# A hybrid decoder block on one core: one value mix ahead of a weight split, a projection tile by halves, compression blocks in other places

## The chip, the cores and the metric

The kernel runs on one core of a Trainium2 chip. A core has a matrix engine (TensorE, PE in the profile), a vector engine (DVE), an activation engine (ACT), a general engine (GpSimd, POOL), and SyncE (SP), which here issues the weight transfers. Each engine runs its own instructions in order, and waits on the others by semaphores. The metric is the device time of one execution in microseconds; the number before is the median of three runs.

## What is computed

One layer of a decoder, for 512 tokens of width 1024, in fp32. A normalised input goes through one wide projection. Its columns feed a sparse attention mixer (queries, three kinds of keys and values), an RWKV-7 recurrence and two gates. Both mixers are projected, merged by the gates, projected again and added; a gated MLP with a short convolution follows.

```python
h = rmsnorm(x, attn_norm_g[l])
proj = h @ w_in[l]
q, k_c, v_c, k_s, v_s, k_w, v_w, nsa_gate, rwkv_in, gate_a, gate_b = jnp.split(proj, IN_SPLITS, axis=-1)
o_a = nsa_mixer(q, k_c, v_c, ...)
o_b = rwkv7_mixer(rwkv_in, ...)
merged = jax.nn.sigmoid(gate_a) * (o_a @ w_proj_a[l]) + jax.nn.sigmoid(gate_b) * (o_b @ w_proj_b[l])
x = x + (merged @ w_out[l]).astype(x.dtype)
h2 = rmsnorm(x, ffn_norm_g[l])
x = x + conv_ffn(h2, ...)
```

Two details matter for the change. In the recurrence every projected column is mixed with that of the token before:

```python
shifted = jnp.pad(p_in, ((0, 0), (1, 0), (0, 0)))[:, :-1]
xl = p_in + (shifted - p_in) * mu
```

And the compression of the attention's keys and values cuts the tokens into overlapping blocks of 32 with a stride of 16 (31 blocks), adds a position embedding to each, and maps the flattened block by a small network:

```python
blocks = blocks + pe[None, None, :, None, :]
flat = blocks.transpose(0, 1, 3, 2, 4).reshape(b, n_cmp, g, CMP_BLOCK * dh)
return jax.nn.gelu(flat @ w1) @ w2
```

## The kernel before

**Weights in two parts.** A product in fp32 is made of three in a reduced format. Each weight tile arrives as `raw` (512 KB, a DMA from SP); ACT copies its high part into `whi` and DVE or POOL subtracts to get the low part `wlo` (`wsplit_`, the subtraction is line 299). The inputs have the parts `hh` and `hl`, and TensorE adds up hh by whi, hl by whi and hh by wlo. `weight_tiles` lists all tiles in the order of their use, with the engine that makes the low part; `wnext` hands out the next one, and in doing so issues the load and the split of the ones behind it. Compression weights (`cmp_w1_*`) are used as they arrive, without a split.

**Order.** Most instructions are written in program order and placed by a scheduler. While `urgent` is filled, the splits get priority. Some stretches (`tc.manual_schedule`) fix the order on the engines they name.

**The stages around the change.** The kernel works through the recurrence's four pairs of heads (`p` = 0 to 3): `front`, `norms`, `receptance`, `values_of`, `values_tok`, `vectors`, `gram`. `values_of(p)` projects the values on TensorE and mixes them with their neighbours (`shift_mix`: ACT scales, then DVE's `stt`, line 137, makes `vx`); `values_tok(p)` turns `vx` into token order by four transposes on TensorE (line 531). `gram(p)` forms products, of which DVE writes the masked result into `AB` (line 128). Between the last pair's `values_of` and `values_tok` TensorE makes the projection of the compressed keys, `kcp`. After the last pair `windows` copies it on ACT into `Dc`, a part of `QK`, and the query projection `dense_tok(512, hh, hl)` follows. This takes four weight tiles of two row blocks each; a tile is multiplied into four PSUM banks, one for each 128 tokens, all high parts first and then all low parts. The banks come from a ring of four (`ps_mm`), shared with what came before.

Meanwhile DVE inverts small triangular matrices in `inv`: four stream transposes (line 614) and a loop of 31 steps (lines 616 to 622), then stream transposes (L723 into `Y1`, which lies in `sg1[:, 1:3]`; L728 from `AB`). TensorE and ACT finish the inverse (`below`, `left`), with the projection of the last keys (`kv_proj(1, 280)`, three tiles) filled in between. `norm_keys(0)` and `rstd` make norms on DVE (rows with `rs_m`, `rs_y`), by which POOL multiplies keys and queries (lines 714 and 773).

**Compression.** `compress` writes blocks `Rk` on DVE (line 128, sg<-QK,prm): for keys and values, two groups and two halves (`jh`), eight writes of 8 by 31 columns, and fills the last column with zero (line 790). Then come four passes `s4` over the first weight, of 16 matmuls each, with other projections between them. The places `sg0` and `sg1`, four strips of 512 columns each, later receive the gates (`siga`). `sg0` shares its memory with `spare`, the split weights of one query tile and one key tile. The keys' blocks lie in `sg1[:, 0:2]` and the values' in `sg1[:, 2:4]`.

Of the kernel before, what the change touches and what calls it, by code (L numbers as in the profile page):

```python
# [23 lines left out]
NT = S // 128  # L24
# [58 lines left out]
def hybrid_block(ctx: ExitStack, tc: tile.TileContext, A: dict, out: bass.AP):  # L83
# [52 lines left out]
    def stt(o, a, s, b, op0=ALU.mult, op1=ALU.add):  # L136
        v.scalar_tensor_tensor(o, a, s, b, op0=op0, op1=op1)  # L137
# [120 lines left out]
            yield from rows(A["w_down"][0], 512 * hf, 512, NF)  # L258

    wtiles = weight_tiles()  # L260
    loads, ahead, late, slots = [], [], [], itertools.count()
    def wload():
        nxt = next(wtiles, None)
        if nxt is not None:
# [17 lines left out]
    def wsplit_():  # L282
        if loads:
            raw, kt, n, eng = loads.pop(0)
            if eng is None:
                ahead.append(raw)
                return
            if type(eng) is tuple:
                eng = eng[1]
                hi, lo = (spare[:, i].rearrange("p (k n) -> p k n", n=n) for i in range(2))  # L290
                act(hi, raw)
            else:
                hi = wp.tile([128, kt, n], F32R, name="whi", tag="whi", bufs=2)
                if late:
                    late.pop()(hi, raw)
                else:
                    act(hi, raw)
                lo = wp.tile([128, kt, n], F32R, name="wlo", tag="wlo", bufs=2)
            eng.tensor_tensor(lo, raw, hi.bitcast(F32), op=ALU.subtract)  # L299
            ahead.append((hi, lo))  # L300

    def wnext(kt, n):
# [100 lines left out]
    def dense_fm(xh, xl, kt=KT):  # L403
        return run(dense_fm_g(xh, xl, kt))
# [25 lines left out]
    def shift_mix(p, m, dst):  # L430
        mu = col("rwkv_mu", m)
        act(dst, p, AF.Copy, scale=omm[:, m:m + 1])
        stt(dst[:, 1:], p[:, :-1], mu, dst[:, 1:])

    def t2(name, bufs=1):
        return tp.tile([128, S], F32, name=name, tag=name, bufs=bufs)
# [84 lines left out]

    def values_of(p):
        vx = t2("vx")
        shift_mix(dense_fm(hh, hl), 8 + p, vx)
        L[p]["vx"] = vx

    def values_tok(p):
# [94 lines left out]
        stt(Tn[:, k + 1:, 0:n], tmv, 1.0, Tn[:, k + 1:, 0:n], ALU.mult, ALU.add)  # L622


    def dense_tok_g(n, xh, xl, kt=KT):
        banks = [mmb() for _ in range(NT)]
        step = 1024 // n
        tiles = [list(range(k0, min(k0 + step, kt))) for k0 in range(0, kt, step)]

        def passes(parts, ts_):  # L630
            for part in range(2):
                for ks, w in parts:
                    for i, k in enumerate(ks):
                        for t in ts_:
                            qs = slice(128 * t, 128 * t + 128)
                            if part == 0:
                                mm(banks[t][:, 0:n], xh[:, k, qs], w[0][:, i], k == 0, False)
                                mm(banks[t][:, 0:n], xl[:, k, qs], w[0][:, i], False, False)
                            else:
                                mm(banks[t][:, 0:n], xh[:, k, qs], w[1][:, i], False, k == kt - 1)  # L640
                    if len(ts_) > 1:
                        yield

        for ks in tiles[:-2]:
            yield from passes([(ks, wnext(len(ks), n))], range(NT))
        last = [(ks, wnext(len(ks), n)) for ks in tiles[-2:]]
        for t in range(NT):
            yield from passes(last, [t])
            if t < NT - 1:
                yield  # L650
        return banks

    def dense_tok(*a, **kw):
        return run(dense_tok_g(*a, **kw))
# [18 lines left out]

    windows(0, kcp)
    urgent.append(1)
    bq = dense_tok(512, hh, hl)
    for t in range(NT):
        act(qn[:, t], bq[t])
        for h in range(H):
# [104 lines left out]


    def compress():
        Rk = [sg1[:, 2 * a:2 * a + 2].rearrange("p m s -> p (m s)").rearrange("p (j g n) -> p j g n", j=16, g=2)
              for a in range(2)]
        for a, s_ in enumerate("kv"):
            v.memset(Rk[a][:, :, :, 31:32], 0.0)  # L790
            r0 = ROWS["cmp_pe_" + s_][0]
            for g in range(2):
                dv = Dc[:, a, g].rearrange("p (n j) -> p j n", j=8)
                for jh in range(2):
                    tt(Rk[a][:, 8 * jh:8 * jh + 8, g, 0:31], dv[:, :, jh:31 + jh],
                       prm[:, r0 + 8 * jh:r0 + 8 * jh + 8, None].to_broadcast([128, 8, 31]), ALU.add)
        cw2, hid, hidT, kcd = (QK[:, o:o + 256] for o in range(3072, 4096, 256))
        cw2 = cw2.rearrange("p (a m d) -> p a m d", a=2, m=2)
        hidT = hidT.rearrange("p (m a n) -> p m a n", m=2, a=2)
        kcd = kcd[0:32].rearrange("p (g a d) -> p g a d", g=2, a=2)  # L800
        kcs = cp.tile([32, 2], F32, name="kcs")
        yield
        hx = mmb()[:, 0:256]
        for s4 in range(4):
            w = [wnext(4, 256) for _ in range(2)]
            for j in range(4):
                for a in range(2):
                    mm(hx[64 * a:64 * a + 64], Rk[a][:, 4 * s4 + j].rearrange("p g n -> p (g n)"), w[a][:, j],
                       s4 + j == 0, s4 + j == 6)
            if s4 == 2:  # L810
                for a, s_ in enumerate("kv"):
                    nc.sync.dma_start(cw2[:, a], A["cmp_w2_" + s_][0].rearrange("(m p) d -> p m d", p=128))
            yield
        act(hid, hx, AF.Square)
        ts(hid, hid, 0.044715, 1.0)
        tt(hid, hid, hx, ALU.mult)
        act(hid, hid, AF.Tanh, scale=math.sqrt(2.0 / math.pi))
        stt(hid, hid, 1.0, hx, ALU.add, ALU.mult)
        yield
        pt = mmb()  # L820
        for m in range(2):
            te.transpose(pt[:, 128 * m:128 * m + 128], hid[:, 128 * m:128 * m + 128], ident)
        act(hidT.rearrange("p m a n -> p (m a n)"), pt[:, 0:256])
        yield
        kc_ps = mmb()
        for g in range(2):
            for m in range(2):
                mm(kc_ps[0:32, 64 * g:64 * g + 64], hidT[:, m, 0, 32 * g:32 * g + 32], cw2[:, 0, m], m == 0, m == 1)
        nc.gpsimd.memset(vcb, 0.0)
        for g in range(2):  # L830
            for e in range(2):
                bs = slice(64 * g + 32 * e, 64 * g + 32 * e + 32)
                for m in range(2):
                    mm(kc_ps[bs, 128:192], hidT[:, m, 1, 32 * g:32 * g + 32], cw2[:, 1, m], m == 0, m == 1)
        for g in range(2):
            for e in range(2):
                bs = slice(64 * g + 32 * e, 64 * g + 32 * e + 32)
                act(vcb[bs, 2 * g + e], kc_ps[bs, 128:192], AF.Copy, scale=0.5)
        for g in range(2):
            act(kcd[:, g, 0], kc_ps[0:32, 64 * g:64 * g + 64], AF.Copy, scale=0.5)  # L840
            act(kcd[:, g, 1], kcd[:, g, 0], AF.Square, accum_out=kcs[:, g:g + 1])
        rstd(kcs, DH)
        for g in range(2):
            ts(kcd[:, g, 1], kcd[:, g, 0], kcs[:, g:g + 1], None)
            ts(kcd[:, g, 0], kcd[:, g, 0], kcs[:, g:g + 1], None)
        yield
        pt = mmb()
        for g in range(2):
            te.transpose(pt[:, 32 * g:32 * g + 32], kcd[:, g].rearrange("p a d -> p (a d)"), ident[0:32, 0:32])
        ptv = pt[:, 0:64].rearrange("p (g n) -> p g n", g=2)  # L850
        act(KC[:, :, 0], ptv, AF.Copy, scale=kg)
        stt(KC[:, :, 1], ptv, kg, KC[:, :, 0].bitcast(F32), ALU.mult, ALU.subtract)
# [366 lines left out]
    units += [(qt, g, (0, 1)) for qt in (1, 0) for g in range(2)]  # L1219
    nfill = [5, 5, 6, 6, 7, 8, 10, 10, 10, 9, 9, 6]  # L1220
    with tc.manual_schedule(engines=KTS):
        behind = (1,2,3,4,5,6,7,8,9)
        scores(units[0], 12)
        scale(units[0])
        comp = compressed(3)
        next(comp)
        scores(units[1], 12)
        for i, u in enumerate(units):
            turns(u)
            if i == 0:  # L1230
                run(comp)
            if i in (4, 8, 10):
                compressed_t(u[0])
            if i + 2 < len(units):
                mid = [lambda: None, functools.partial(scale, units[i + 1])] if i + 1 in behind else [lambda: None, lambda: None]
                if i == 0:
                    mid.insert(0, functools.partial(compressed_t, 3))
                scores(units[i + 2], nfill[i], mid)
                if i + 2 not in behind:
                    scale(units[i + 2])  # L1240
            else:
                filler(nfill[i])
            if i in (1, 5, 7):
                run(compressed({1: 2, 5: 1, 7: 0}[i]))
            values(u)
        filler(100)
# [155 lines left out]
```

## Time and profile before

| | |
|---|---|
| runs | 834.2, 834.1, 833.83 us |
| median | 834.1 us |
| profiled execution | 833.78 us, of which 831.9 us are the span of the trace |
| granted TensorE clock | 1.0 over the whole span |
| TensorE (PE) busy | 823.2 us |
| DVE, ACT, POOL busy | 514.4, 406.4, 51.5 us |

The span goes from the first to the last instruction of the trace; what lies around it, 1.9 us, is start and end. A row of a timeline has the start, the duration, the engine and line, the operation, output and inputs by their names, the tile and the type, and how many of the kind it holds; in brackets stand the idle time before it and what ended that. Matmuls overlap, so the distance between two starts tells more than the duration.

### The profile page before, as it was taken

Reading aid. Unit: us, or ns where it says so; the run is one execution under the profiler, and the core shown is the slowest. Engines: PE = TensorE matmul, PEld = TensorE weight load, DVE = VectorE, ACT = ScalarE, POOL = GpSimd, SP = SyncE. Lnnn points to the kernel's source line nnn. Section 1 sums busy time; section 2 is a strip of 40 time slices with the busy share of each in tenths; the row PEclk is TensorE's granted clock in tenths of the full one; section 3 lists DMA queues with packets and bytes.
Section 4 is the critical chain, followed back from the end, with each engine's and each line's share of the span. In section 5 each row is a group of like instructions: output and inputs, shape, how many; then the busy total and the mean of one; then the engine's idle time right before and its main releaser. Section 6 shows DMA issues by size and latency. Waiting matters only on the chain.

```text
span 831.9 us, 12894 instructions
## 1 busy us (share of the span) xinstructions
PE 823.2 (99%) x5107; PEld 669.9 (81%) x5107; DVE 514.4 (62%) x1006; ACT 406.4 (49%) x793; POOL 51.5 (6%) x67
## 2 busy tenths in 40 slices
PE   8999999999999999999999999999999999999998
PEld 7777778987777887787788988888888888888886
DVE  6577779974565878787665576556665556323222
ACT  6766655554455777685334554444444444221220
POOL 6100020140000200011000000000000000000000
PEclk9999999999999999999999999999999999999999
DMA  8432222246372310001275033333323332223421
GB/s 247 110 84 58 76 76 77 69 128 185 102 128 77 86 42 14 26 27 34 81 258 148 1 114 89 101 103 101 97 86 96 101 102 102 88 90 114 139 76 51
DMA packets 109400, 78.73 MB, mean 95 GB/s; under 512 B 3877, under 2 KB 98012, under 8 KB 109340
## 3 DMA queue, kind: packets, MB, share of 16 engines
q1 hardware_dynamic: 106800, 73.92, 30.2%
q10 hardware_dynamic: 1196, 2.55, 0.9%
q0 software_dynamic: 1344, 1.45, 0.8%
q8 instruction: 40, 0.66, 0.3%
q14 instruction: 20, 0.16, 0.1%
HBM read 74.56 MB, written 2.29 MB: 92 GB/s over the span
## 4 chain that ended last, share of the span: by engine, by line
PE 91%; DVE 5%; ACT 2%; issue 1%; DMA 0%; DVEq 0%; ACTq 0%
PE ps_mm L122 81%; PE ps_a L122 5%; PE ps_b L122 2%; PE ps_b L1196 1%; PE ps_mm L1196 1%; DVE AB L128 0%; DMA xt<-in_x_dram 0%; DVE P L1163 0%; DVE sC L128 0%; DVE wlo L299 0%; ACT P L125 0%; ACT L125 0%; ACT UV L125 0%; DVE P L132 0%; DVE PTs L1108 0%
## 5 line engine op out<-in xcount | busy, mean ns | idle before, releaser
L299 DVE TENSOR_TENSOR wlo<-raw,whi 128x1024 fp32r<-128x1024 f32 (+1 forms) x111 | 131.5, 1185 | 184.3 <-PE ps_mm L122 160.0
L122 PE MATMUL ps_mm<-hh,whi 128*128 128x512 f32 (+1 forms) x624 | 242.4, 391 | 0.5 <-DVE hl L137 0.5
L122 PE MATMUL ps_mm<-hl,whi 128*128 128x512 f32 (+1 forms) x624 | 240.2, 387 | 0.0
L125 ACT ACTIVATE whi<-raw 128x1024 fp32r<-128x1024 f32 (+3 forms) x124 | 123.3, 996 | 158.1 <-PE ps_mm L122 142.6
L122 PE MATMUL ps_mm<-hh,wlo 128*128 128x512 f32 (+1 forms) x624 | 152.1, 384 | 0.0
L122 PEld LDWEIGHTS ps_mm<-hh,whi 128*128 128x128 f32 x624 | 117.3, 188 | 27.2 <-issue 1.0
L122 PEld LDWEIGHTS ps_mm<-hl,whi 128*128 128x128 f32 x624 | 117.4, 188 | 23.0 <-issue 1.0
L122 PEld LDWEIGHTS ps_mm<-hh,wlo 128*128 128x128 f32 x624 | 115.1, 188 | 23.5
L122 PE MATMUL ps_mm<-whi,aT 128*128 128x512 f32 x352 | 84.5, 390 | 0.0
L122 PEld LDWEIGHTS ps_mm<-whi,aT 128*128 128x128 f32 x352 | 65.9, 188 | 14.3 <-issue 0.4
L137 DVE SCALAR_TENSOR_TENSOR cgv<-ps_mm,cw,cgv 128x511 f32<-128x511 f32 (+1 forms) x88 | 65.4, 746 | 1.6
L125 ACT ACTIVATE cgv<-ps_mm,cw 128x512 f32<-128x512 f32 x44 | 34.2, 780 | 23.3 <-PE ps_mm L122 23.3
L122 PE MATMUL ps_mm<-wlo,aT 128*128 128x512 f32 x176 | 44.3, 389 | 0.0
L125 ACT ACTIVATE aT<-cgv 128x512 fp32r<-128x512 f32 x22 | 13.9, 632 | 56.8 <-DVE cgv L128 56.8
L125 ACT ACTIVATE P<-P,nm 128x512 f32<-128x512 f32 (+3 forms) x64 | 35.4, 554 | 12.2 <-DVE nm L1163 12.0
L122 PEld LDWEIGHTS ps_mm<-wlo,aT 128*128 128x128 f32 x176 | 33.0, 188 | 6.9
L125 ACT ACTIVATE cgv<-cgv 128x512 f32<-128x512 f32 x22 | 13.9, 632 | 41.3 <-DVE cgv L137 41.2
L299 POOL TENSOR_TENSOR wlo<-raw,whi 128x512 fp32r<-128x512 f32 (+3 forms) x13 | 20.7, 1593 | 200.9 <-PE ps_mm L122 132.2
L1163 DVE CUSTOM_DVE_ANT_0 P<-ps_a,AB 128x512 f32<-128x512 f32 (+3 forms) x64 | 29.3, 485 | 4.1 <-PE ps_a L122 4.0
L128 DVE TENSOR_TENSOR x<-x,ps_mm 128x512 f32<-128x512 f32 (+1 forms) x17 | 11.0, 655 | 22.8 <-PE ps_mm L122 20.6
L128 DVE TENSOR_TENSOR aT<-cgv,aT 128x512 fp32r<-128x512 f32 x22 | 15.3, 693 | 14.7 <-ACT aT L125 14.7
L125 ACT ACTIVATE QK<-ps_mm 128x64 f32<-128x64 f32 (+5 forms) x56 | 14.9, 309 | 18.4 <-PE ps_mm L122 18.3
(357 smaller groups left out, 1209.9 us busy)
## 6 DMA issues: line engine op xcount, KB each, us to landing
raw<-in_w_up_dram SPq DMA_DIRECT2D x44, 512.0 KB, 3.7
raw<-in_w_in_dram SPq DMA_DIRECT2D x38, 512.0 KB, 3.8
raw<-in_w_down_dram SPq DMA_DIRECT2D x22, 512.0 KB, 3.5
raw<-in_w_out_dram SPq DMA_DIRECT2D x8, 512.0 KB, 3.6
xt<-in_x_dram SPq DMA_DIRECT2D x4, 512.0 KB, 4.0
raw<-in_cmp_w_v_dram SPq DMA_DIRECT2D x4, 512.0 KB, 3.8
raw<-in_w_proj_b_dram SPq DMA_DIRECT2D x8, 256.0 KB, 2.6
raw<-in_w_proj_a_dram SPq DMA_DIRECT2D x8, 256.0 KB, 2.6
```

Of the source, the lines that this page charges most:

```text
L122: te.matmul(o, lhsT=l, rhs=r, start=start, stop=stop)
L125: sc.activation(o, i, f, **kw)
L128: v.tensor_tensor(o, a, b, op=op)
L137: v.scalar_tensor_tensor(o, a, s, b, op0=op0, op1=op1)
L299: eng.tensor_tensor(lo, raw, hi.bitcast(F32), op=ALU.subtract)
L1163: v.tensor_tensor_reduce(out=P[:, i], in0=sp[:, N * (i - i0):N * (i - i0) + N], in1=BT[:, h, 384 - 128 * qt:512], scale=-1.0, scalar=-NEG, ...
L1196: te.transpose(pt[:, 128 * i:128 * i + 128], P[:, 4 * x + i, 128 * k:128 * k + 128], ident)
```

## The change

Three things are changed. First, `shift_mix` returns its last instruction, and the weight split that comes after the values of the last pair gets an order edge behind it: on DVE `vx` stands ahead of the subtraction for the first query tile. Second, the first tile of the query projection is multiplied by two token tiles and then by the other two, high and low parts each time, instead of by all four. Third, the compression blocks have other places: the keys' halves in `sg0[:, 1]` and `sg0[:, 3]`, the values' in `sg0[:, 2]` and `sg1[:, 0]`, and each half has its own fill. By the built programs, two of the eight block writes stay in the inverse loop, and six, with three fills of 128 by 16, stand right behind the four transposes of L728 and ahead of the norms. The orders on ACT, POOL and SP are the same as before. A tuple in the attention loop has a new name.

```diff
-    loads, ahead, late, slots = [], [], [], itertools.count()
+    loads, ahead, late, behind, slots = [], [], [], [], itertools.count()
...
-            eng.tensor_tensor(lo, raw, hi.bitcast(F32), op=ALU.subtract)
+            low = eng.tensor_tensor(lo, raw, hi.bitcast(F32), op=ALU.subtract)
+            if behind:
+                tc.add_manual_dep(low.ins, behind.pop().ins.name, mybir.DependencyInfo(
+                    mybir.DependencyClass.NoSync, mybir.DependencyReason.DATA), reason="values of the last pair first")
...
-        stt(dst[:, 1:], p[:, :-1], mu, dst[:, 1:])
+        return v.scalar_tensor_tensor(dst[:, 1:], p[:, :-1], mu, dst[:, 1:], op0=ALU.mult, op1=ALU.add)
...
-        shift_mix(dense_fm(hh, hl), 8 + p, vx)
+        mixed = shift_mix(dense_fm(hh, hl), 8 + p, vx)
+        if p == NH2 - 1:
+            behind.append(mixed)
...
-    def dense_tok_g(n, xh, xl, kt=KT):
+    def dense_tok_g(n, xh, xl, kt=KT, halves=False):
...
-        for ks in tiles[:-2]:
-            yield from passes([(ks, wnext(len(ks), n))], range(NT))
+        for j, ks in enumerate(tiles[:-2]):
+            parts = [(ks, wnext(len(ks), n))]
+            for ts_ in ([range(2), range(2, NT)] if halves and j == 0 else [range(NT)]):
+                yield from passes(parts, ts_)
...
-    bq = dense_tok(512, hh, hl)
+    bq = dense_tok(512, hh, hl, halves=True)
...
-        Rk = [sg1[:, 2 * a:2 * a + 2].rearrange("p m s -> p (m s)").rearrange("p (j g n) -> p j g n", j=16, g=2)
-              for a in range(2)]
+        Rk = [[w.rearrange("p (j g n) -> p j g n", j=8, g=2) for w in ws]
+              for ws in ((sg0[:, 1], sg0[:, 3]), (sg0[:, 2], sg1[:, 0]))]
         for a, s_ in enumerate("kv"):
-            v.memset(Rk[a][:, :, :, 31:32], 0.0)
+            for w in Rk[a]:
+                v.memset(w[:, :, :, 31:32], 0.0)
...
-                    tt(Rk[a][:, 8 * jh:8 * jh + 8, g, 0:31], dv[:, :, jh:31 + jh],
+                    tt(Rk[a][jh][:, :, g, 0:31], dv[:, :, jh:31 + jh],
...
-                    mm(hx[64 * a:64 * a + 64], Rk[a][:, 4 * s4 + j].rearrange("p g n -> p (g n)"), w[a][:, j],
+                    mm(hx[64 * a:64 * a + 64], Rk[a][s4 // 2][:, 4 * (s4 % 2) + j].rearrange("p g n -> p (g n)"), w[a][:, j],
```

More of the change, by code (lines that the diff above doesn't have):

```diff
@@ L1221, in hybrid_block @@
     with tc.manual_schedule(engines=KTS):
-        behind = (1,2,3,4,5,6,7,8,9)
+        after_next = (1,2,3,4,5,6,7,8,9)
         scores(units[0], 12)
@@ L1234, in hybrid_block @@
             if i + 2 < len(units):
-                mid = [lambda: None, functools.partial(scale, units[i + 1])] if i + 1 in behind else [lambda: None, lambda: None]
+                mid = [lambda: None, functools.partial(scale, units[i + 1])] if i + 1 in after_next else [lambda: None, lambda: None]
                 if i == 0:
@@ L1238, in hybrid_block @@
                 scores(units[i + 2], nfill[i], mid)
-                if i + 2 not in behind:
+                if i + 2 not in after_next:
                     scale(units[i + 2])
```

## The prediction

> **What bounds the kernel.** I read the page's first part, then TensorE's timeline around each place that the change touches, then DVE, ACT and POOL at the same moments. TensorE is the bound:
>
> ```profile
> span 831.9 us, 12894 instructions
> ## 1 busy us (share of the span) xinstructions
> PE 823.2 (99%) x5107; PEld 669.9 (81%) x5107; DVE 514.4 (62%) x1006; ACT 406.4 (49%) x793; POOL 51.5 (6%) x67
> ```
>
> TensorE is busy for 823.2 of 831.9 us, so faster work elsewhere brings nothing by itself. Only the moments in which TensorE waits count. "Idle before" understates them, since pipelined matmuls overlap, so I take the distance from one start to the next and compare it with the same step where nothing is late. The first such place is the transposes of the last pair's values, against eight matmuls of the same kind 14 us earlier, behind which other transposes stand that were not late:
>
> ```profile
> 101.44 1.99 PE L122 MATMUL ps_mm<-hh,wlo 128*128 128x512 f32 x8
> 103.36 0.27 PE L562 MATMUL ps_b<-kc,bh 64*128 64x64 f32 x1
> ...
> 115.04 1.97 PE L122 MATMUL ps_mm<-hh,wlo 128*128 128x512 f32 x8
> 117.28 0.44 PE L531 MATMUL ps_b<-kc,vx 128*128 128x128 f32 x2 [0.26 <-DVE vx L137]
> ```
>
> The undisturbed step takes 103.36 - 101.44 = 1.92 us, this one 117.28 - 115.04 = 2.24. The wait is 0.32 us (the bracket shows 0.26 of it), released by DVE's vx. The second place is the first pass over the compression weights:
>
> ```profile
> 176.20 0.80 PE L122 MATMUL ps_mm<-wlo,hh 128*128 128x280 f32 x5
> ...
> 179.67 0.65 PE L122 MATMUL ps_mm<-raw,sg 128*64 128x256 f32 x2
> 180.51 1.94 PE L122 MATMUL ps_mm<-raw,sg 128*64 128x256 f32 x14 [0.19 <-DVE sg L128]
> 182.38 0.39 PE L122 MATMUL ps_mm<-whi,hh 128*128 128x280 f32 x1
> ...
> 197.22 1.95 PE L122 MATMUL ps_mm<-raw,sg 128*64 128x256 f32 x16
> 199.10 0.50 PE L122 MATMUL ps_mm<-hh,whi 128*128 128x512 f32 x1
> ```
>
> A later pass of the same 16 matmuls goes from 197.22 to 199.10, 1.88 us; this one from 179.67 to 182.38, 2.71. The wait is 0.83 us, of which the bracket shows only 0.19. Its releaser is the block that DVE writes into sg.
>
> **Part one: vx ahead of the split.** What DVE does before the transposes:
>
> ```profile
> 115.34 1.22 DVE L299 TENSOR_TENSOR wlo<-raw,whi 128x1024 fp32r<-128x1024 f32 x1
> 116.48 0.74 DVE L137 SCALAR_TENSOR_TENSOR vx<-ps_mm,prm,vx 128x511 f32<-128x511 f32 x1
> 118.83 0.69 DVE L128 TENSOR_TENSOR BO<-ps_a,vx 128x512 f32<-128x512 f32 x1 [1.61 <-PE ps_a L122]
> ```
>
> The split (wlo, 1.22 us) stands ahead of vx (0.74). In the other order vx ends near 116.1 instead of 117.22, ahead of the transposes' undisturbed start at 115.04 + 1.92 = 116.96. The whole 0.32 goes; the least I allow is the bracket's 0.26. The split moves back by 0.74 - less than BO's 1.61 us of idle time - and ends near 117.3. Its reader is the query projection, which starts after 121: hidden by four microseconds of recurrence products. No instruction is added; behind the new order edge on DVE stands only the split.
>
> **Part two: the query projection's first tile by two token tiles.** The same 24 matmuls go in another order; the third and fourth banks are touched first at places 13 and 15 instead of 7 and 11. The rows there, first TensorE's, then the DVE evacuation that frees banks two and three, then ACT's that frees the fourth:
>
> ```profile
> 119.21 0.22 PE L562 MATMUL ps_a<-kc,bh 64*128 64x64 f32 x1
> 119.57 0.37 PE L122 MATMUL ps_b<-AR,bh 64*128 64x128 f32 x1
> ...
> 122.12 0.40 PE L122 MATMUL ps_mm<-whi,hh 128*128 128x512 f32 x1
> 122.70 0.50 PE L122 MATMUL ps_mm<-whi,hh 128*128 128x512 f32 x1 [0.18 <-DVE AB L128]
> ...
> 123.52 0.39 PE L122 MATMUL ps_mm<-whi,hh 128*128 128x512 f32 x1
> ...
> 124.44 0.40 PE L122 MATMUL ps_mm<-whi,hh 128*128 128x512 f32 x1
> ```
>
> ```profile
> 121.97 1.28 DVE L128 TENSOR_TENSOR AB<-ps_mm,kc 128x512 f32<-128x512 f32 x2
> ```
>
> ```profile
> 121.75 1.06 ACT L125 ACTIVATE spare<-raw 128x1024 fp32r<-128x1024 f32 x1 [1.12 <-issue]
> 122.71 1.54 ACT L125 ACTIVATE QK<-ps_mm 64x256 f32<-64x256 f32 x4
> ```
>
> The wait that exists is at the second bank: 122.70 - 122.12 = 0.58, against a pace of 1.92 / 8 = 0.24, so 0.34 us. The new order keeps that matmul in fourth place, so the wait stays. Bank three is free at 121.97 + 1.28 = 123.25 and wanted at 123.52; bank four is free at 122.71 + 1.54 = 124.25 and wanted at 124.44. Neither is late, so this part is worth **0**. It becomes a cover: TensorE now comes 0.32 earlier, and if ACT's copy at 121.75 does not come earlier with it (what released it is not shown), bank four would be late by 0.32 - 0.19 = 0.13 us in the old order, and not in the new one. Value 0, bounds 0 to 0.13 of loss avoided, so the sum is not touched either way. The low half of the weight is now wanted at the ninth matmul instead of the seventeenth, after 123, and is done at 117.3.
>
> **Part three: the compression blocks' places.** Eight block writes of one kind stand on DVE:
>
> ```profile
> L128 DVE TENSOR_TENSOR sg<-QK,prm 128x248 f32<-128x248 f32 x8 | 5.0, 642 | 0.0
> ```
>
> ```profile
> 166.29 8.06 DVE L728 STREAM_TRANSPOSE AB<-inv 32x1024 f32<-32x1024 f32 x4
> 174.38 1.37 DVE L134 TENSOR_SCALAR rs_m<-kss 128x8 f32<-128x8 f32 x1
> 175.67 0.17 DVE L134 TENSOR_SCALAR rs_m<-qss 128x32 f32<-128x32 f32 x1
> ```
>
> Before, four of them run in the inverse loop and four follow the chain of norms, because their place is that of the inverse's transposes, which TensorE and ACT still use. After, two run in the loop and six stand right behind the four transposes (end 174.35), ahead of the norms, with three small fills that I bound by a small norm operation, 0.17 each. Six times 0.642 and three times 0.17 make 4.4 us. They start at the earliest at 174.35 - 0.32 - 2 x 0.642 (the two that leave the loop) = 172.8, at the latest at 174.35, so they end at 177.2 to 178.7. TensorE wants them at 179.67 - 0.32 = 179.35. Even the late end is 0.6 us ahead, and the **0.83 goes whole**.
>
> What is late next: the norms begin 2.8 to 4.3 us later than now and no longer beside the split, whose company cost them 1.2 (1.37 - 0.17); their end, which releases POOL, moves from 178.0 to 181 at most. POOL's rows:
>
> ```profile
> 174.33 1.39 POOL L299 TENSOR_TENSOR wlo<-raw,whi 128x560 fp32r<-128x560 f32 x1 [4.99 <-ACT AB L125]
> 178.02 2.65 POOL L714 TENSOR_TENSOR QK<-QK,kss 128x128 f32<-128x128 f32 x4 [2.30 <-DVE kss L137]
> 180.63 4.04 POOL L773 TENSOR_TENSOR QK<-QK,qss 128x512 f32<-128x512 f32 x4
> 192.65 1.48 POOL L714 TENSOR_TENSOR QK<-QK,kss 128x128 f32<-128x128 f32 x4 [7.97 <-DVE kss L137]
> ```
>
> POOL's eight multiplies (2.65 + 4.04) then end before 188, and its next work starts at 192.65: hidden, worth 0.
>
> The price that is new is POOL's split at 174.33. TensorE uses its result from the fourth matmul of the five at 176.20, at 176.20 + 3 x 0.13 = 176.6 (0.13 is half of 512-wide pace by 280 columns: 0.24 x 280 / 512), and 0.32 earlier after the first gain, 176.3. Today it runs beside small norms; after, beside block writes. Two rows show what that does: the same four POOL multiplies take 2.65 us beside block writes (178.02) and 1.48 alone (192.65), a factor of 1.8, while DVE's own 1.37 for a small operation beside the split, 0.17 otherwise, shows DVE giving way. If DVE gives way, the split costs TensorE nothing: released 0.32 earlier, it ends near 175.4, and with one block write ahead of it at 176.0. If POOL is slowed by 1.8, it ends at 174.0 + 2.5 = 176.5, 0.2 late. I take 0.1, between ends that are close.
>
> The Trainium skill ("SBUF — State Buffer", section "SBUF: two separate sides") says that DVE and GpSimd share one port pair under an exclusive lock, which whoever starts first holds for its whole instruction, DVE taking part also with two SBUF inputs against a GpSimd operation that reads SBUF. The 1.37 against 0.17 agrees; the slowed multiplies, beside which DVE's block writes were not slowed, agree only in part. By the rule POOL waits for one write, and the sum would be 0.1 larger than mine.
>
> **The sum.** -0.32 - 0.83 + 0.1 = -1.05 us. The profiled run took 833.78 (span 831.9), which becomes 832.7. The median of the runs is 834.1, 0.3 above the profiled one, and becomes **833.0**.
>
> **Rivals.** *More gain:* the other waits near these places go too, because DVE's and ACT's rows there come earlier by more than TensorE's. The step from 119.21 to 119.57 (0.36; two products of 64 columns are 0.06 at the same pace: 0.30 us) and the 0.34 at 122.70 would add 0.64, and with the 0.1 not paid: -1.8, 832.3. For it: a changed order on an engine often lets more than one wait go. Against: what releases them is work that follows the same TensorE transposes and so moves with them.
>
> *Given back at a transfer.* A later weight copy of ACT waits for its transfer:
>
> ```profile
> 197.55 1.06 ACT L125 ACTIVATE whi<-raw 128x1024 fp32r<-128x1024 f32 x1 [6.97 <-DMA raw<-in_w_in_dram]
> ```
>
> It ends at 198.61; TensorE wants it at 199.10. If the landing does not come earlier with TensorE, the 0.49 of slack holds and 1.05 - 0.49 = 0.56 is given back: -0.5, 833.6. Against: the buffer of that transfer is released by TensorE, so it is issued earlier too.
>
> *Slower:* POOL's split is starved by the six block writes until the last has ended. It then ends at 177.2 + 1.39 = 178.6 to 180.1, TensorE stalls for 2.3 to 3.8 us in the keys' projection (less the 0.1 of the sum), and the change costs +1.1 to +2.6: 835.2 to 836.7. It turns slower from the point where the split ends after 176.3 + 1.15 = 177.4. For it: the 2.65 against 1.48. Against: the multiplies at 178.02 did run beside the writes, at more than half pace.
>
> **Chances.** Forecast 0.56; more gain 0.24; given back 0.10; slower 0.10. The range goes from 832.1 to 834.3. A fifth of a per cent of 834.1, 1.7 us, is about what a measurement of this kernel can tell from no change: faster means under 832.4, slower over 835.8. The more-gain case lies around the first bound and mostly below it, the starved case around the second: faster 0.28, same 0.65, slower 0.07.
>
> **What would show it.** Right: vx ends before the eight matmuls do, and the step to the transposes takes 1.92; the first compression pass takes 1.88; the matmul at bank two keeps its 0.34. Wrong: POOL's split lengthened beyond 2.3 us or started late, with TensorE's gap inside the five at 176.20; a block write after TensorE's first compression matmul; a new gap ahead of 199.10 with ACT's copy as its releaser.

## The result and the profile after

| | before | after |
|---|---|---|
| median of 22 runs each | 833.83 us (833.49 to 834.2) | 832.61 us (832.28 to 832.93) |
| ratio, 95% interval | | 0.9985 (0.9979 to 0.999) |
| span of the profiled execution | 831.9 us | 830.7 us |

The change saves 1.22 us, 0.15%, inside the predicted range; the predicted saving was 1.05. Every run of the changed kernel lies below every run of the kernel before. The median is 0.4 us below the predicted 833.0, but 0.27 of that is the starting point: the prediction went from 834.1, the median of three runs, and the 22 runs have 833.83. The page of the changed kernel, span and busy time:

```profile
span 830.7 us, 12893 instructions
## 1 busy us (share of the span) xinstructions
PE 821.3 (99%) x5107; PEld 669.1 (81%) x5107; DVE 514.4 (62%) x1008; ACT 406.2 (49%) x793; POOL 50.7 (6%) x67
```

DVE's busy time is the same to the tenth of a microsecond, with two instructions more, and TensorE's count is the same: no work was taken away. (TensorE's busy time rests on modelled ends and cannot be read to a microsecond.) TensorE's timeline (start, duration, line, operation) shows that two waits are gone:

```profile
115.09 1.98 PE L122 MATMUL ps_mm<-hh,wlo 128*128 128x512 f32 x8
116.90 0.60 PE L536 MATMUL ps_b<-kc,vx 128*128 128x128 f32 x4
...
121.69 0.40 PE L122 MATMUL ps_mm<-whi,hh 128*128 128x512 f32 x1
122.27 0.50 PE L122 MATMUL ps_mm<-whi,hh 128*128 128x512 f32 x1 [0.19 <-DVE AB L128]
122.60 0.63 PE L122 MATMUL ps_mm<-whi,hl 128*128 128x512 f32 x2
...
175.74 0.80 PE L122 MATMUL ps_mm<-wlo,hh 128*128 128x280 f32 x5
...
179.22 1.95 PE L122 MATMUL ps_mm<-raw,sg 128*64 128x256 f32 x16
181.09 0.40 PE L122 MATMUL ps_mm<-whi,hh 128*128 128x280 f32 x1
...
197.87 0.50 PE L122 MATMUL ps_mm<-hh,whi 128*128 128x512 f32 x1
```

I read the gain by subtracting the starts of the same instructions in the two traces. At the eight low-part matmuls the changed kernel is 0.05 us later (115.09 against 115.04; the start of the first projection varies more than that, from 13.37 to 13.71 over all traces of this document). At 122.12, now 121.69, it is 0.43 earlier; at 176.20, now 175.74, 0.46; at 182.38, now 181.09, 1.29; at 199.10, now 197.87, 1.23. So the vx part brought 0.46 + 0.05 = about 0.5 us by then, the compression part 1.29 - 0.46 = 0.83, and 0.06 was lost again by 199.

DVE and POOL in the same stretch:

```profile
115.38 0.75 DVE L436 SCALAR_TENSOR_TENSOR vx<-ps_mm,prm,vx 128x511 f32<-128x511 f32 x1
116.04 1.22 DVE L299 TENSOR_TENSOR wlo<-raw,whi 128x1024 fp32r<-128x1024 f32 x1
...
173.32 3.81 DVE L128 TENSOR_TENSOR sg<-QK,prm 128x248 f32<-128x248 f32 x5
176.57 0.07 DVE L798 MEMSET sg<- 128x16 f32 x1
177.05 0.63 DVE L128 TENSOR_TENSOR sg<-QK,prm 128x248 f32<-128x248 f32 x1
```

```profile
173.88 1.78 POOL L299 TENSOR_TENSOR wlo<-raw,whi 128x560 fp32r<-128x560 f32 x1 [5.00 <-ACT AB L125]
180.03 1.47 POOL L721 TENSOR_TENSOR QK<-QK,kss 128x128 f32<-128x128 f32 x4 [4.36 <-DVE kss L137]
181.46 4.05 POOL L780 TENSOR_TENSOR QK<-QK,qss 128x512 f32<-128x512 f32 x4
191.71 1.47 POOL L721 TENSOR_TENSOR QK<-QK,kss 128x128 f32<-128x128 f32 x4 [6.20 <-DVE kss L137]
```

vx ends at 115.38 + 0.75 = 116.13, 0.77 us ahead of its transposes. The last block write ends at 177.05 + 0.63 = 177.68, 1.54 ahead of the first compression matmul at 179.22. POOL's split, 1.39 us long before, now takes 1.78 and ends at 175.66; TensorE wants it at 175.74 + 3 x 0.13 = 176.13.

### The profile page after: what moved, and what is told of

It reads as the page before. It is cut to its first block, busy times and chain, and to the rows that moved or that the text cites. A ratio compares the mean times of both kernels' runs of the same rounds, so it can differ in the third digit from the quotient of the medians.

```text
span 830.7 us, 12893 instructions
## 1 busy us (share of the span) xinstructions
PE 821.3 (99%) x5107; PEld 669.1 (81%) x5107; DVE 514.4 (62%) x1008; ACT 406.2 (49%) x793; POOL 50.7 (6%) x67
## 4 chain that ended last, share of the span: by engine, by line
PE 95%; DVE 3%; ACT 1%; DMA 0%; issue 0%; DVEq 0%; ACTq 0%
PE ps_mm L122 84%; PE ps_a L122 5%; PE ps_b L122 2%; PE ps_b L1204 1%; PE ps_mm L1204 1%; DMA xt<-in_x_dram 0%; DVE P L1171 0%; DVE sC L128 0%; ACT P L125 0%; DVE P L132 0%; PE ps_b L536 0%; PE ps_b L567 0%; DVE PTs L1116 0%; PE ps_a L1016 0%; PE ps_b L203 0%
```

## The experiments

All were compared with the kernel before in the same job; differences are those of the medians. "Full change" is the changed kernel, at 832.61 us. It was measured in a job of its own, and the median of the kernel before moved from 833.83 to 833.97 us between the jobs, so a difference to the full change is good to about 0.1 us.

**One part at a time.** Each of the first three kernels keeps one part of the change; the fourth leaves only the halves out. The diffs here and below are against the changed kernel.

```diff
 e1, e3, e4:
-    bq = dense_tok(512, hh, hl, halves=True)
+    bq = dense_tok(512, hh, hl)
 e2, e3:
-        if p == NH2 - 1:
-            behind.append(mixed)
 e1, e2:
-        Rk = [[w.rearrange("p (j g n) -> p j g n", j=8, g=2) for w in ws]
-              for ws in ((sg0[:, 1], sg0[:, 3]), (sg0[:, 2], sg1[:, 0]))]
+        Rk = [sg1[:, 2 * a:2 * a + 2].rearrange("p m s -> p (m s)").rearrange("p (j g n) -> p j g n", j=16, g=2)
+              for a in range(2)]
...
```

> Only the order edge that puts the last pair's vx ahead of the weight split. My theory: the three parts add up, and this one is worth the whole distance that TensorE gained at the transposes of vx: in the changed kernel the step from the eight low-part matmuls to them takes 116.90 - 115.09 = 1.81 us, before 117.28 - 115.04 = 2.24, so 0.43 us less time and the compression pass keeps its 2.71 us. By the prediction's own reference step (1.92) it would be 0.32. Rival: the 0.11 above that comes with another part (the halves), and this kernel shows a step of 1.92. Second rival: what TensorE gains here is lost again at bank four of the query projection, which is 0.13 us late without the halves, so 0.30.

> Only the query projection's first tile by two token tiles. My theory: no bank beyond the second was late, so the time is that of before within 0.1 us, and the wait at the second bank keeps its 0.34 us. Rival: the new order takes away a wait in the 24 matmuls that the rows did not show, and the time falls by 0.1 to 0.4 us.

> Only the new places of the compression blocks. My theory: the first compression pass takes 1.88 us instead of 2.71, and the time falls by 0.83 us; POOL's split beside the block writes takes about 1.8 instead of 1.39 us and is in time. Rival: POOL's split, which here is wanted 0.4 us later than in the full change, or a later transfer gives part back, and the time falls by 0.3 to 0.6.

> The full change without the halves. My theory: same as the full change, 1.2 us less than before, since in the changed kernel ACT's copy for bank four moved with TensorE. Rival, the halves as a cover: bank four is late by about 0.13 us, seen as a gap in the first 24 matmuls, and the time falls by 1.1 only.

| kernel | median, us | before in the same job | difference |
|---|---|---|---|
| e1, vx ahead of the split | 833.4 | 833.92 | -0.52 |
| e2, halves | 833.9 | 833.92 | -0.02 |
| e3, places of the blocks | 833.13 | 833.92 | -0.79 |
| e4, full change without the halves | 832.62 | 833.92 | -1.30 |

The parts add up: 0.52 + 0.79 = 1.31 is what the two give together. The intervals of the ratios (0.9985 to 1.0003 for e1, 0.9982 to 0.9999 for e3) are about as wide as the effects. Still, every run of e1 (at most 833.54) and of e3 (at most 833.36) lies below every run of the kernel before in that job (at least 833.56). Where the time went, the traces show. TensorE's timeline of e1:

```profile
115.18 1.98 PE L122 MATMUL ps_mm<-hh,wlo 128*128 128x512 f32 x8
117.00 0.60 PE L536 MATMUL ps_b<-kc,vx 128*128 128x128 f32 x4
...
179.34 0.65 PE L122 MATMUL ps_mm<-raw,sg 128*64 128x256 f32 x2
180.14 1.94 PE L122 MATMUL ps_mm<-raw,sg 128*64 128x256 f32 x14 [0.15 <-DVE sg L128]
182.01 0.40 PE L122 MATMUL ps_mm<-whi,hh 128*128 128x280 f32 x1
```

The step to the transposes is 117.00 - 115.18 = 1.82 without the halves, so the 0.11 above the predicted 0.32 belongs to the vx part, and the first rival falls; with 0.52 us gained, the second falls too. The compression pass still waits: 182.01 - 179.34 = 2.67. Of e3:

```profile
117.47 0.66 PE L534 MATMUL ps_b<-kc,vx 128*128 128x128 f32 x4 [0.27 <-DVE vx L436]
...
179.87 1.95 PE L122 MATMUL ps_mm<-raw,sg 128*64 128x256 f32 x16
181.75 0.40 PE L122 MATMUL ps_mm<-whi,hh 128*128 128x280 f32 x1
```

Here the wait on vx is back (0.27) and the pass takes 181.75 - 179.87 = 1.88; with 0.79 us gained, nothing much was given back. The halves alone change nothing, and with the rest, their absence (e4) costs nothing either. The cover that I allowed them was not needed, because ACT's copy in the changed kernel had moved with TensorE:

```profile
121.31 1.06 ACT L125 ACTIVATE spare<-raw 128x1024 fp32r<-128x1024 f32 x1 [1.12 <-issue]
```

121.75 became 121.31, 0.44 earlier like TensorE's own rows, so bank four kept its slack. In e4, which has no cover, that copy starts at 121.21, and from the fifth matmul of the tile on the steps are the usual 0.23: the third and fourth banks are not late.

**The two waits that were left.** The rival of more gain said that these go too. They did not by themselves: in the changed kernel the second bank still waits (122.27 - 121.69 = 0.58). The next three kernels take them away. e5 exchanges the banks in the last pair's gram:

```diff
-            ptr = [mmb(), mmb()] if c0 else [pb(), pa()]
+            ptr = [mmb(), mmb()] if (c0 > 0) != (p == NH2 - 1) else [pb(), pa()]
```

e6 gives the second bank its own turn; e7 has both edits:

```diff
-            for ts_ in ([range(2), range(2, NT)] if halves and j == 0 else [range(NT)]):
+            for ts_ in ([range(1), range(1, 2), range(2, NT)] if halves and j == 0 else [range(NT)]):
```

> The full change, and in the last pair's gram the first four chunks go to banks of the ring of four (ps_mm) and the last four to the pair ps_a, ps_b, the other way round than before. It tests the rival of more gain: whether the two waits that the change left can go. My theory: the products need not wait for ACT's copies of the values (118.79 to 119.14 in the changed kernel, 0.35 with 0.06 of work: 0.3 us), and DVE frees the two banks of the ring first, so the matmul at the second bank of the query projection (0.34 us) is not late either: 0.6 us less than the full change, 1.85 less than before. Rival: the waits only move, TensorE meets the same DVE chain at the next bank, and 0.3 or nothing is gained.

> The full change, with the query projection's first tile taken by one, one and two token tiles instead of two and two. My theory: the second bank, free 0.34 us after TensorE wants it in fourth place, is wanted in seventh place, three matmuls or 0.69 us later, so that wait goes: 0.34 us less than the full change, 1.55 less than before. Rival: what the halves did already (a new order of the same 24 matmuls, worth nothing) holds for this too, because the low part or another bank is late instead: no gain.

> The full change with the two edits of the runs before together. My theory: both take away the same wait at the second bank, so together they give what the exchanged gram banks give alone, 0.6 us less than the full change. Rival: each takes away a part of it, and together they give 0.3 us more than either.

| kernel | median, us | before in the same job | difference | ratio, 95% interval |
|---|---|---|---|---|
| e5, gram banks exchanged | 831.8 (831.5 to 831.95) | 833.93 | -2.13 | 0.9974 (0.9964 to 0.9984) |
| e6, first tile by 1, 1, 2 | 832.11 (832.01 to 832.32) | 833.93 | -1.82 | 0.9978 (0.9969 to 0.9987) |
| e7, both | 831.77 (831.59 to 831.94) | 833.93 | -2.16 | 0.9974 (0.9964 to 0.9984) |

TensorE's timeline of e5, and below it DVE's first evacuation; then TensorE's timeline of e6 where it comes to the second bank:

```profile
118.63 0.22 PE L567 MATMUL ps_a<-kc,bh 64*128 64x64 f32 x1
118.69 1.11 PE L122 MATMUL ps_mm<-AR,bh 64*128 64x128 f32 x16
...
121.20 0.39 PE L122 MATMUL ps_mm<-whi,hh 128*128 128x512 f32 x1
121.43 0.40 PE L122 MATMUL ps_mm<-whi,hl 128*128 128x512 f32 x1
121.66 0.39 PE L122 MATMUL ps_mm<-whi,hh 128*128 128x512 f32 x1
```

```profile
119.83 1.29 DVE L128 TENSOR_TENSOR AB<-ps_mm,kc 128x512 f32<-128x512 f32 x2 [0.90 <-PE ps_mm L122]
```

```profile
122.19 0.62 PE L122 MATMUL ps_mm<-wlo,hh 128*128 128x512 f32 x2
122.65 0.39 PE L122 MATMUL ps_mm<-whi,hh 128*128 128x512 f32 x1
```

In e5 the products follow the transposes after 0.06 us instead of 0.35, and the matmuls of the query projection follow each other at 0.23 us without a gap, since DVE empties the ring's banks first, at 119.83 instead of 121.53 in the changed kernel. The expected 0.6 us below the full change became 832.61 - 831.8 = 0.81: the wait at the second bank was worth more than its 0.34, as e6 shows, which takes away that one alone (from 122.19 to 122.65 are two steps of 0.23) and gains 832.61 - 832.11 = 0.50 instead of 0.34. In the traces the 24 matmuls of the tile take 6.06 us in the changed kernel (121.12 to 127.18) and 5.62 in e6 (121.14 to 126.76), 0.44 less. I had counted the step at the fourth matmul and not the next one, in the changed kernel 122.27 to 122.60, 0.33 where 0.23 is the pace. e7 gives what e5 gives, so both edits take the same wait and my expectation holds. e5 is the version that beats both kernels: all its runs are below all runs of the changed kernel.

**The slack of the blocks.** e8 does every key block's write twice, with the same values:

```diff
-                    tt(Rk[a][jh][:, :, g, 0:31], dv[:, :, jh:31 + jh],
-                       prm[:, r0 + 8 * jh:r0 + 8 * jh + 8, None].to_broadcast([128, 8, 31]), ALU.add)
+                    for _ in range(1 + (a == 0)):
+                        tt(Rk[a][jh][:, :, g, 0:31], dv[:, :, jh:31 + jh],
+                           prm[:, r0 + 8 * jh:r0 + 8 * jh + 8, None].to_broadcast([128, 8, 31]), ALU.add)
```

> The full change, with every block write of the keys done twice (four more writes on DVE, same values). It measures the slack of the blocks. My theory: in the changed kernel the last write ends at 177.68 and TensorE's first pass starts at 179.22, 1.54 us later; four more writes at a pace of 0.55 us and two small norm operations of 0.1 that now stand between end at 180.1, so TensorE waits about 0.9 us and the time is 0.9 us above the full change. POOL's split gets its turn between two writes, after one of them at most, and ends no later than in the changed kernel. Rival, the slower side of the prediction: the split is starved by the longer row of writes, ends after 179, and TensorE loses some 3 us in the keys' projection, ahead of the compression pass.

It took 833.44 us (833.37 to 833.73), 0.83 above the full change. DVE, then TensorE:

```profile
173.53 6.09 DVE L128 TENSOR_TENSOR sg<-QK,prm 128x248 f32<-128x248 f32 x9
...
179.64 0.63 DVE L128 TENSOR_TENSOR sg<-QK,prm 128x248 f32<-128x248 f32 x1
```

```profile
179.36 0.65 PE L122 MATMUL ps_mm<-raw,sg 128*64 128x256 f32 x2
180.33 1.94 PE L122 MATMUL ps_mm<-raw,sg 128*64 128x256 f32 x14 [0.33 <-DVE sg L128]
```

The last write ends at 180.27 and TensorE goes on at 180.33: the wait of the kernel before is back. Its price follows from the slack: the last write ends 2.59 us later than in the changed kernel, TensorE comes 0.14 later, and 2.59 - 0.14 - 1.54 = 0.91; the pass takes 182.20 - 179.36 = 2.84 instead of 1.87, 0.97 more. POOL's split was not starved by ten writes in a row; it took its turn after the first:

```profile
174.02 1.39 POOL L299 TENSOR_TENSOR wlo<-raw,whi 128x560 fp32r<-128x560 f32 x1 [4.99 <-ACT AB L125]
```

**POOL's split beside the writes.** e9 gives this split to DVE:

```diff
-            yield from rows(w_in, O_KW, 280, eng=pool_)
+            yield from rows(w_in, O_KW, 280, eng=[pool_, pool_, v])
```

> The full change, with the last low-part split of the keys' projection (128 by 560) made by DVE instead of POOL; on DVE it stands behind the block writes and the norms. It tests two things. First, whether POOL's split is what lengthens one block write to 1.71 us in the changed kernel, where the others take about 0.6: my theory, the two engines take turns, an instruction at a time, so without the split every write takes about 0.6, and the six of them end 1.1 us earlier, near 176.6. Rival: the long write is long for another reason and stays. Second, the price of a late low part, the slower side of the prediction: the norms end near 179.0, the split near 179.7, and TensorE wants the result at 175.74 + 3 x 0.13 = 176.1, so it waits 3.5 us and the time is 3.5 us above the full change, near 836.1. Rival: TensorE has other work or DVE comes earlier, and it costs under 1 us.

It took 838.08 us (837.97 to 839.63), 5.47 above the full change. First the block writes, by a view of the tile in a window around them (count, shortest, median and longest in ns), in the changed kernel and then in e9:

```profile
L128 DVE TENSOR_TENSOR sg<-QK,prm x6: 587/614/1710, 173.3 to 177.1; 128x248 f32<-128x248 f32 x6
```

```profile
L128 DVE TENSOR_TENSOR sg<-QK,prm x6: 601/626/654, 173.5 to 176.2; 128x248 f32<-128x248 f32 x6
```

Without POOL's split no write is long, and the last ends at 176.17 + 0.62 = 176.79 instead of 177.68. So the 1.71 us were one write that waited for the split. Second, TensorE and its granted clock by a view of stretches (the last three columns are TensorE's granted clock, the DMA share and GB/s):

```profile
175.88 0.55 PE L122 MATMUL ps_mm<-wlo,hh 128*128 128x280 f32 x3
179.91 0.52 PE L122 MATMUL ps_mm<-wlo,hh 128*128 128x280 f32 x2 [3.47 <-DVE wlo L299]
```

```profile
181.40:184.40 3.00, 3.00 (x16) 2.74 (x16) 0.12 (x1) 0.40 (x3) 3.00 (x4) 0.52 0.50 170
184.40:187.00 2.60, 2.60 (x21) 1.65 (x21) 0.00 (x0) 1.27 (x7) 0.79 (x1) 0.90 0.00 0
```

The fourth low-part matmul waits as expected: 3.47 us by the bracket, and from start to start 179.91 - 175.88 - 3 x 0.13 = 3.64. What I had not expected is the rest, about 1.8 us: after the wait TensorE's clock is granted at half for about 3.4 us. A finer view of stretches has 1.00 from 178 to 181.5, 0.50 from 181.6 to 184.9 and 1.00 from 185 on. Half the clock for 3.4 us loses 1.7 us. In the two longest of its five runs, 839.15 and 839.63 us, the mean granted clock was 0.996 instead of 0.998; 0.002 of 836 us is again 1.7 us, but no trace of these runs was kept.

## Why the prediction came out right, step by step

**vx ahead of the split:** the mechanism is right, the size too small: 0.32 predicted, 0.43 at the step itself (2.24 - 1.81). The four transposes behind it also go 0.05 faster (117.77 - 117.28 = 0.49 before, 117.34 - 116.90 = 0.44 after), so up to the matmul behind them it is 0.48, near the 0.52 of e1. The reference step was chosen wrongly, and the sign that the prediction gave, a step of 1.92, was not what came. The 1.92 us end at transposes with a 64-row operand, and the step to such an operation takes 0.11 longer even where nothing is late. The changed kernel has both kinds, the one at 115.09 to 116.90 above (1.81) and this one:

```profile
101.49 1.99 PE L122 MATMUL ps_mm<-hh,wlo 128*128 128x512 f32 x8
103.41 0.27 PE L567 MATMUL ps_b<-kc,bh 64*128 64x64 f32 x1
```

The kernel before already had the right reference, eight such matmuls with 128-row ones behind them:

```profile
125.82 1.98 PE L122 MATMUL ps_mm<-wlo,hh 128*128 128x512 f32 x8
127.63 0.39 PE L122 MATMUL ps_mm<-whi,hh 128*128 128x512 f32 x1
```

This step is 1.81. Why the 64-row operand costs 0.11 was not tried.

The split, moved back, cost nothing, as worked out.

**The halves at 0:** right, by e2 and e4. Also the wait at the second bank stayed, as forecast; only its full worth, 0.44 us in the trace of e6 and 0.50 in its runs, was not seen.

**The compression blocks at 0.83:** right, 2.71 - 1.87 = 0.84 in the trace, 0.79 in the runs of e3. The last write was to end between 177.2 and 178.7 and ended at 177.68. The norms were to release POOL by 181 and did at 180.03; POOL ended at 181.46 + 4.05 = 185.5, far ahead of 191.71.

**POOL's split at 0.1:** the term was mis-sized; it cost 0. I had read the multiplies that took 2.65 us beside block writes as an engine slowed by 1.8, with the split to end at 176.5. The runs show turns: the split waits for the write that is running (1.78 - 1.39 = 0.39 us in the changed kernel, none in e8), runs at its own speed, and the next write waits for it. The rows that had led to the factor fit this too. In the kernel before, the first two writes and the first two multiplies, one by one:

```profile
178.01 0.64 DVE L128 TENSOR_TENSOR sg<-QK,prm 128x248 f32<-128x248 f32 x1
178.59 0.65 DVE L128 TENSOR_TENSOR sg<-QK,prm 128x248 f32<-128x248 f32 x1
```

```profile
178.02 0.82 POOL L714 TENSOR_TENSOR QK<-QK,kss 128x128 f32<-128x128 f32 x1 [2.30 <-DVE kss L137]
178.81 0.65 POOL L714 TENSOR_TENSOR QK<-QK,kss 128x128 f32<-128x128 f32 x1
```

The ends alternate: 178.65 (write), 178.84 (multiply), 179.24 (write), 179.46 (multiply). A multiply ends about 0.2 us after a write and a write 0.4 after a multiply, while one alone shows 0.40 and about 0.62. So at each change the two overlap by about 0.2 us, an estimate from these rows, and each multiply waits for one write. The 1.8 was therefore one wait for each short instruction and no factor to put on a long one. Turns are the rule of the Trainium skill ("SBUF — State Buffer", "SBUF: two separate sides") that the prediction weighed: an exclusive lock held for the whole instruction. This case's traces agree, with 1.71 us for the blocked write against 0.61, but for that overlap, and the sum by that rule, 0.1 larger, was the better one.

**The rivals.** More gain: not seen, since both waits stood until e5 moved the banks. Given back at a transfer: almost none; at 199.10, now 197.87, the shift is 1.23 of 1.29. ACT's copy at 197.55 starts at 196.39 in the changed kernel, 1.16 earlier, so the transfer moved nearly as TensorE did; what took the 0.06 was not tried. Slower through a starved split: fell with e8, where ten writes did not hold it up. The point from which a late split decides is real, though: in e9 TensorE stops at the very matmul that the prediction named. The price that this rival put on a stall was too low, since it left out the clock: e9's stall of 3.64 us cost 5.47.

The sum with the measured terms is -0.48 - 0.84 + 0 = -1.32, of which 0.06 is lost again by 199, so -1.26, against -1.22 in the medians and -1.2 in the spans. The forecast of -1.05 missed on the same side twice, by 0.16 at vx and by 0.1 at POOL's split; no error hid another.

## What to carry to other kernels

Where TensorE is 99% busy, look for the few steps whose start-to-start distance is longer than that of the same step elsewhere, and take as the reference a step with the same shapes on both sides; the bracketed idle time showed 0.19 of a wait of 0.83. What is late there is often not slow but stands in the wrong place of another engine's row, or writes to memory that is still in use: a new place or a new order cost nothing here. When a wait is found at one bank, look also at who empties it and in which order, as that was worth more here (0.8 us, with the wait in front of the products) than reordering the reader's matmuls (0.5).

## What the hardware showed

DVE and POOL took turns, an instruction at a time, in these elementwise operations on SBUF, with an overlap of about 0.2 us at each change: a write of 0.61 us became 1.71 beside a POOL split of 1.39, and in e9, where DVE's own split came first (179.11 to 179.85), the first of POOL's four multiplies took 0.98 us where one alone shows 0.40:

```profile
179.13 0.98 POOL L721 TENSOR_TENSOR QK<-QK,kss 128x128 f32<-128x128 f32 x1 [10.11 <-DVE kss L137]
```

In e9 an idle TensorE paid twice: after the idle 3.47 us its clock was granted at 0.50 for about 3.4 us, which made the stall of 3.64 us cost 5.47. The Trainium skill ("TensorE: Matmul & The Clock Gate", "Part 1: The HAM clock gate") has the clock fall to half after an idle window of about 3.4 us. The trace agrees as to the length. The moment is another matter: the clock fell near 181.5, when TensorE had been at work again for 1.6 us. The waits in the traces of the other kernels, at most 1.7 us long (in e8, 6 us after the start), left it at 1.0; no trace here has an idle time between 1.7 and 3.47 us.
